# One state-space mixer: another order for the last subtractions, merged parameter loads, and three small moves

## The chip, the cores and the metric

The kernel runs on one core of a Trainium2 chip. The metric is the device time of one execution in microseconds (us), lower is better. The core has four engines that matter here: PE (TensorE, matrix products; its weight loads are listed apart as PEld), DVE (VectorE), ACT (ScalarE) and POOL (GpSimd). SP (SyncE), ACT and POOL also issue DMA transfers, which 16 DMA engines carry out. Each engine executes its own instructions in one fixed order; semaphores tie the engines together.

## The reference

One inference step of a small streaming encoder with two layers, width D = 1024, over 1024 prompt positions without history and 64 sample positions with a carried state. Each layer is a token mixer between RMS norms, then a gated feed-forward net with a causal depthwise convolution. Layer 0 mixes with sliding-window attention, layer 1 with a diagonal complex state-space model (S5), which is the part that the change touches:

```python
def s5_mixer(h, h0_re, h0_im, lam_re, lam_im, log_dt, b_re, b_im, c_re, c_im, d_skip, w_glu, b_glu):
    ...                       # u: h by 64 groups of 16 channels, state of 64 complex numbers a group
        xr = jnp.einsum('blgi,gpi->blgp', u_blk, bbr)      # and xi with bbi: inputs of the state
        ...                                                # the carried state enters at the first position
        _, _, sr, si = lax.associative_scan(_affine_combine, (ar, ai, xr, xi), axis=1)
        y = jnp.einsum('blgp,gip->blgi', sr, cr) - jnp.einsum('blgp,gip->blgi', si, ci)
    ...
    z = jax.nn.gelu(y + d_skip * h)
    ag = z @ w_glu + b_glu
    out = ag[..., :D_MODEL] * jax.nn.sigmoid(ag[..., D_MODEL:])
    return out, hr, hi
```

All of it is float32. The outputs are both activations, the attention cache rows, the final states and the last convolution rows.

## The kernel before, in words

The 1088 positions lie on the free axis, in three blocks of 384, 384 and 320 columns; the width is eight tiles of 128 partitions, kt = 0 to 7. A float32 product is made of three products of a high and a low part: high x low, high x high, low x high (`mm3`, lines 420 to 422; in the GLU line 1701). For a weight tile ACT copies the high part (line 406) and DVE subtracts it from the raw tile to get the low part (line 407); raw tiles have two buffers, and a new load (lines 383, 389) waits until both have read the old one. The order of every engine and of SP's queue is written out by hand in a table of numbers, `PINS`, and made binding by `pin`: an instruction that is not ready holds up all behind it on its engine.

**The mixer** (`ssm`) runs over 32 pairs of groups q, two to a batch except for the first two and the last two. The parameters of two pairs make one tile t of 16 (`pm`; `pm0` for t = 0 and 6), loaded by SP in `load`, one transfer of 522 KB for each pair. A batch does:

- PE, line 1506: the inputs of the state from U (the normed activations by groups, four tiles, scaled by DVE at line 1440) into `p1`;
- ACT, lines 1514 and 1518: a copy of sines `sc`, and the decays `rd` (mask times a number);
- DVE and POOL: `wk` is the state's work tile. DVE multiplies (1539, 1545), adds (1546), scans (1557), multiplies (1560, 1561); POOL zeroes the first column (1538) and copies the carried state `h0` in (1543) before line 1546;
- PE, lines 1569 and 1575: the direct part and the output of the states into `p3`;
- ACT, line 1583: `p3` into `ys`; after four pairs ACT's queue stores `ys` to memory (1589), SP loads it back transposed as `yf` (1595), ACT makes z by GELU (1609, 1612) and its high part `zh` (1620).

For the two batches of t = 0 (q = 0 and 1), line 1571 has PE do an idle product (`fill`, line 427) beside; it writes spare columns of a `p1` bank and nobody reads it.

**The end of the mixer.** The low parts `zl` of z (line 1636, function `lower`) are subtracted on DVE: 24 subtractions, eight tiles kt times three blocks. `lows` makes those of kt 0 to 5, after the low parts of two held weight tiles. `fo`, line 1649, sums the final state, and POOL stores it (1650).

**The GLU** (`tile_`) has eight output tiles m, for three blocks each; `pb` and `pa` are the PSUM sums of gate and value, from six buffers. For m = 0 the products come in four steps, each for all three blocks: high x high of kt 0 to 4; the products of kt 0 to 4 with a low part; kt 5 and 6; kt 7. Then the sigmoid on ACT (1716) and the product on DVE (1717) empty the two sums. Beside it POOL loads (1661), DVE adds and subtracts (1665 to 1668) and POOL stores (1669) sums of weights for the next net (`sj`), for which the small tiles of `t4` (five slots, shared by `ys`, `yf`, `z`, `sg` and `sj`) are used.

Of the kernel before, what the change touches and what calls it, by code (L numbers as in the profile page):

```python
# [203 lines left out]
class Core:  # L204
# [1237 lines left out]
    def ssm(self, after):  # L1442
# [4 lines left out]
        with tc.tile_pool(name="ss", bufs=1) as sp:  # L1447
# [47 lines left out]
            def batch(qs):  # L1495
# [91 lines left out]
                if qs[-1] % 4 == 3:  # L1587
# [33 lines left out]
                    if kt < 6:  # L1621
                        zs[kt] = z
                        return
# [266 lines left out]
```

## Time and profile before

| | |
|---|---|
| median of three runs | 2237.05 us (2235.64 to 2237.27) |
| profiled execution: its own time | 2237.79 us |
| its span | 2236.0 us |
| mean granted PE clock | 0.992 |
| instructions | 35979 |
| mixer, from the first line-1539 product to the last scan step | 1185.0 to 1268.2 us |
| GLU, from its first product | 1272.0 us on |

Rows of a timeline have the start in us from the span's start, the duration, engine, line, operation, the tile written and those read, the number of instructions in the row and, in brackets, how long the engine stood before it and what released it. A window row has busy time and number of instructions by engine, then the granted PE clock, the mean share of the 16 DMA engines that was busy (it can read over 1), and GB/s. Matmul ends are modelled, so their starts are more exact than their ends.

### The profile page before, as it was taken

What the parts mean: (1) busy time and instruction counts of PE and PEld (TensorE: products, weight loads), DVE (VectorE), ACT (ScalarE), POOL (GpSimd) and SP (SyncE); (2) the same over time, 40 slices, a digit from 0 to 9 for tenths busy, and PEclk for the clock granted to TensorE, in tenths of its full rate; (3) what the DMA queues carried; (4) which work ended last, traced back from release to release, by engine and by line L of the source; (5) the groups of instructions that cost most, each with busy time, mean ns of one, the idle gap of its engine ahead of it and who ended that gap; (6) DMA issues with size and microseconds to landing.
All of it is one profiled execution on the core that took longest, in us unless ns stands there. A gap on an engine that the chain in (4) does not pass through costs nothing.

```text
span 2236.0 us, 35979 instructions
## 1 busy us (share of the span) xinstructions
PE 2190.7 (98%) x13867; PEld 2116.8 (95%) x13867; DVE 1646.0 (74%) x2886; ACT 1046.0 (47%) x1865; POOL 423.1 (19%) x504
## 2 busy tenths in 40 slices
PE   9999999999999999999998899999999999999999
PEld 9987799999999999999986789999999999999998
DVE  8688648989878787767767765397977777677763
ACT  6256756422333332555543821263544445455543
POOL 4322005100122424001102244151021111110000
PEclk9999999999999999999999989999999999999999
DMA  5010015656255565887749878251378686578773
GB/s 208 26 30 21 20 62 177 234 202 211 91 152 173 194 206 173 287 272 232 248 172 354 255 271 301 103 180 63 113 260 277 225 293 229 197 271 307 224 252 101
DMA packets 208123, 428.47 MB, mean 192 GB/s; under 512 B 23312, under 2 KB 114224, under 8 KB 205008
## 3 DMA queue, kind: packets, MB, share of 16 engines
q1 hardware_dynamic: 175648, 326.56, 44.2%
q0 software_dynamic: 23984, 95.12, 12.0%
q10 hardware_dynamic: 8320, 4.49, 0.8%
q8 instruction: 109, 1.79, 0.3%
q14 instruction: 62, 0.51, 0.1%
HBM read 297.75 MB, written 128.37 MB: 191 GB/s over the span
## 4 chain that ended last, share of the span: by engine, by line
PE 73%; DMA 10%; DVE 9%; ACT 3%; issue 3%; POOL 1%; SPq 0%; ACTq 0%; DVEq 0%; POOLq 0%
PE mm L420 17%; PE mm L421 17%; PE mm L422 17%; PE pa L1701 4%; PE pb L1701 4%; DMA raw<-in_w_down 2%; PE po L1037 2%; DMA jw<-in_w_down 1%; PE tps L1030 1%; PE sps L1007 1%; PE p L1575 1%; DVE whl L407 1%; PE gq L420 1%; PE gq L422 1%; PE gq L421 1%
## 5 line engine op out<-in xcount | busy, mean ns | idle before, releaser
L420 PE MATMUL mm<-hl,whl 128*128 128x384 f32 (+1 forms) x1960 | 643.1, 329 | 3.1 <-DVE hl L504 2.0
L421 PE MATMUL mm<-hh,whl 128*128 128x384 f32 (+1 forms) x1960 | 643.1, 328 | 0.0
L422 PE MATMUL mm<-hh,whl 128*128 128x384 f32 (+1 forms) x1960 | 640.7, 328 | 0.4 <-DVE whl L407 0.4
L420 PEld LDWEIGHTS mm<-hl,whl 128*128 128x128 f32 x1960 | 368.5, 188 | 5.6 <-DVE hl L504 3.1
L422 PEld LDWEIGHTS mm<-hh,whl 128*128 128x128 f32 x1960 | 368.4, 188 | 0.9 <-DVE whl L407 0.7
L421 PEld LDWEIGHTS mm<-hh,whl 128*128 128x128 f32 x1960 | 368.7, 188 | 0.1
L407 DVE TENSOR_TENSOR whl<-raw,whl 128x1024 fp32r<-128x1024 f32 x201 | 250.6, 1249 | 138.8 <-ACT whl L406 138.5
L406 ACT ACTIVATE whl<-raw 128x1024 fp32r<-128x1024 f32 x201 | 212.0, 1058 | 282.7 <-PE mm L422 128.6
L420 PE MATMUL mm<-gt,whl 128*128 128x384 f32 (+1 forms) x968 | 317.1, 328 | 0.8 <-DVE y L843 0.5
L421 PE MATMUL mm<-gt,whl 128*128 128x384 f32 (+1 forms) x968 | 316.1, 327 | 0.0
L422 PE MATMUL mm<-gt,whl 128*128 128x384 f32 (+1 forms) x968 | 315.8, 327 | 0.0
L420 PEld LDWEIGHTS mm<-gt,whl 128*128 128x128 f32 x968 | 181.7, 188 | 1.5 <-DVE y L843 0.9
L421 PEld LDWEIGHTS mm<-gt,whl 128*128 128x128 f32 x968 | 181.7, 188 | 0.0
L422 PEld LDWEIGHTS mm<-gt,whl 128*128 128x128 f32 x968 | 181.6, 188 | 0.0
L373 DVE TENSOR_TENSOR whl<-raw,whl 128x1024 fp32r<-128x1024 f32 x84 | 96.5, 1154 | 75.2 <-ACT whl L372 74.8
L372 ACT ACTIVATE whl<-raw 128x1024 fp32r<-128x1024 f32 x84 | 82.7, 987 | 102.1 <-DMA raw<-sd 42.3
L648 ACT ACTIVATE t<-u,ppt 128x1090 f32<-128x1090 f32 x88 | 114.2, 1298 | 34.3 <-DVE u L747 23.5
L649 DVE SCALAR_TENSOR_TENSOR t<-u,ppt,t 128x1090 f32<-128x1090 f32 x88 | 125.9, 1431 | 5.3 <-ACT t L648 3.8
L650 DVE SCALAR_TENSOR_TENSOR t<-u,ppt,t 128x1090 f32<-128x1090 f32 x88 | 121.9, 1385 | 0.4
L640 DVE TENSOR_TENSOR u<-rb,mm 128x384 f32<-128x384 f32 (+1 forms) x164 | 80.6, 503 | 34.1 <-PE mm L422 29.3
L663 ACT ACTIVATE t<-t 128x1090 f32<-128x1090 f32 x44 | 49.1, 1116 | 119.1 <-DVE t L650 119.0
L793 DVE TENSOR_TENSOR gt<-gr,gt 128x768 fp32r<-128x768 f32 (+2 forms) x106 | 90.4, 880 | 10.9 <-ACT gt L792 10.2
(400 smaller groups left out, 4072.1 us busy)
## 6 DMA issues: line engine op xcount, KB each, us to landing
raw<-in_w_up SPq DMA_DIRECT2D x88, 512.0 KB, 4.4
raw<-in_w_down SPq DMA_DIRECT2D x74, 512.0 KB, 4.5
raw<-sd SPq DMA_DIRECT2D x40, 512.0 KB, 4.5
sj<-in_w_up POOLq DMA_DIRECT2D x68, 256.0 KB, 5.9
su<-sj POOLq DMA_DIRECT2D x34, 512.0 KB, 5.4
raw<-su SPq DMA_DIRECT2D x34, 512.0 KB, 4.7
pm<-prm SPq DMA_DIRECT2D x32, 522.0 KB, 8.4
gr<-td SPq DMA_DIRECT2D x40, 384.0 KB, 5.5
```

The lines of the kernel that those rows point to most:

```text
L372: nc.scalar.activation(w[:, 0], raw, AF.Copy)
L373: nc.vector.tensor_sub(w[:, 1], raw, w[:, 0].bitcast(F32))
L406: x = [nc.scalar.activation(w[:, 0], raw, AF.Copy)]
L407: low = lambda: nc.vector.tensor_sub(w[:, 1], raw, w[:, 0].bitcast(F32))
L420: nc.tensor.matmul(out, w[:, 0, sl], xl, start=start, stop=False, skip_group_check=more)
L421: nc.tensor.matmul(out, w[:, 0, sl], xh, start=False, stop=False, skip_group_check=more)
L422: self.last_mm = nc.tensor.matmul(out, w[:, 1, sl], xh, start=False, stop=stop, skip_group_check=more)
L648: nc.scalar.activation(t, u[:, 0:T + 2], AF.Identity, bias=cb(m), scale=cw(0, m))
L649: nc.vector.scalar_tensor_tensor(t, u[:, 1:T + 3], cw(1, m), t, op0=ALU.mult, op1=ALU.add)
L650: self.last_conv = nc.vector.scalar_tensor_tensor(t, u[:, 2:T + 4], cw(2, m), t, op0=ALU.mult, op1=ALU.add)
L793: nc.vector.tensor_sub(x[:, 1, u], raw, x[:, 0, u].bitcast(F32))
L1701: nc.tensor.matmul(ps[:, :n], w[:, e, k * P:(k + 1) * P], x[b][:, k], start=k == 0 and j == 0, stop=k == KD - 1 and j == 2)
```

## The change

Five edits, all in the mixer and its hand-written order.

1. The low parts of tile kt = 7 stood first among DVE's last subtractions; they stand last now, behind the 18 of kt 0 to 5, the sum `fo` and kt 6.
2. From t = 4 on, the parameters of two pairs come in one load of 1044 KB: 12 loads in place of 24.
3. The initial state h0 gets a tile of its own in a pool that is open from the kernel's start, instead of one in the mixer's pool.
4. On ACT the four decays of the first two batches' tiles stand behind the two small copies of lines 1421 and 1422.
5. The two idle products of line 427 are left out.

From line 1469 on the changed kernel's lines are one higher than before, from the middle of `batch` (1577) three lower, and from `lower` (1630) on one lower. The tables of numbers change in most of their rows, since fewer instructions are numbered, and are cut here.

```diff
@@ PINS @@
...
@@ load @@
-                for e in range(2):
-                    got[t] = nc.sync.dma_start(pm[:, e], self.prm[:, 2 * t + e])
+                k = 1 if t < 4 else 2
+                for e in range(0, 2, k):
+                    got[t] = nc.sync.dma_start(pm[:, e:e + k], self.prm[:, 2 * t + e:2 * t + e + k])
@@ ssm @@
-            h0 = sp.tile([P, NPR, 2], F32, name="h0")
+            h0 = self.small.tile([P, NPR, 2], F32, name="h0", bufs=1)
             nc.gpsimd.dma_start(h0, a["s_h0"])
@@ batch @@
-                    f = self.fill(p1s[-1][:, 0, 2 * NC_:], 1, 512 - 2 * NC_, x) if t == 0 else None
...
-                                if f is not None:
-                                    self.order(x, f)
-                                    f = None
...
                     if kt < 6:
                         zs[kt] = z
                         return
+                    yield
                     if kt < 7:
+                        lows()
+                    else:
                         yield
-                        lows()
                     for b in range(3):
                         x = lower(b, kt, z)
```

The rows of the following lists are instructions in the order of one engine: line, operation, tile written and tiles read with their buffer numbers, size, and the semaphores waited for. First DVE's order at the end of the mixer, before. `whl` is a weight tile of the GLU; `z_12521` is kt 7, `zs_11974`, `zs_12152` and `z_12378` hold kt 0 to 5 two by two, and `zl_12042`, `zl_12045`, `zl_12048` are blocks 0, 1 and 2:

```order
L407 TENSOR_TENSOR whl_12425<-raw_12423,whl_12425 128x1024 [waits DMAHW6_49]
L1636 TENSOR_TENSOR zl_12042<-z_12521,zh_12041 128x384 [waits Activation_49]
L1636 TENSOR_TENSOR zl_12045<-z_12521,zh_12044 128x384 [waits Activation_49]
L1636 TENSOR_TENSOR zl_12048<-z_12521,zh_12047 128x320 [waits Activation_49]
L1636 TENSOR_TENSOR zl_12042<-zs_11974,zh_12041 128x384 x2
L1636 TENSOR_TENSOR zl_12042<-zs_12152,zh_12041 128x384
L1636 TENSOR_TENSOR zl_12042<-z_12378,zh_12041 128x384 x2
```

The same place with the change, where kt 7 is `z_12507`, kt 6 `z_12501` and kt 4 and 5 are `z_12364`:

```order
L407 TENSOR_TENSOR whl_12411<-raw_12409,whl_12411 128x1024 [waits DMAHW2_49]
L1635 TENSOR_TENSOR zl_12031<-zs_11964,zh_12030 128x384 x2
L1635 TENSOR_TENSOR zl_12031<-zs_12139,zh_12030 128x384 x2
L1635 TENSOR_TENSOR zl_12031<-z_12364,zh_12030 128x384 [waits Activation_49]
L1635 TENSOR_TENSOR zl_12034<-zs_11964,zh_12033 128x384 x2
...
L1648 TENSOR_TENSOR fo_12539<-fin_11554 128x128 [waits Pool_49]
L1635 TENSOR_TENSOR zl_12031<-z_12501,zh_12030 128x384 [waits Activation_49]
...
L1635 TENSOR_TENSOR zl_12031<-z_12507,zh_12030 128x384 [waits Activation_49]
```

The wait for the last tile moved from the head of the 24 to its end. Next POOL's order at the mixer's start, before and then with the change (`h0` carried state, `mask` the tile that the decays are made from, `wk` the first batches' work tiles):

```order
L1487 DMA h0_11554<-in_s_h0 128x64 [waits DMAHW0_49,DVE_49,DMAHW5_49,PE_49,DMAHW7_49,Activation_49,Pool_49]
L1491 MEMSET mask_11557 128x138
L1538 MEMSET wk_11571 128x2
...
L1492 MEMSET mask_11557 128x1 [waits Pool_49]
L1493 MEMSET mask_11557 128x1
L1543 COPY wk_11571<-h0_11554 128x2 [waits DMASW6_49,DVE_49]
```

```order
L1488 DMA h0_11552<-in_s_h0 128x64
L1492 MEMSET mask_11555 128x138 [waits DMAHW0_49,DVE_49,DMAHW5_49,PE_49,DMAHW7_49,Activation_49,Pool_49]
L1539 MEMSET wk_11569 128x2
...
L1493 MEMSET mask_11555 128x1 [waits Pool_49]
L1494 MEMSET mask_11555 128x1
L1544 COPY wk_11569<-h0_11552 128x2 [waits DMASW6_49,DVE_49]
```

The wait for the end of the layer boundary moved from the load to the memset behind it. Last, ACT's order around the second store of `ys`, before and then with the change; the numbers at the semaphores DMAHW are those that SP's and ACT's transfers count up in turn:

```order
L1583 ACTIVATE ys_11784<-p3_11820 128x2x137 [waits PE_49]
L1589 DMA yd_11520<-ys_11784 128x8x137 [waits DMAHW2_49,Activation_49]
L1514 ACTIVATE sc_11863<-pm0_11590 128x2x138 [waits DMAHW7_49,DMAHW6_49,DVE_49]
L1514 ACTIVATE sc_11863<-pm0_11590 128x2x138
L1518 ACTIVATE rd_11864<-mask_11557,rho_296 128x276 x2
```

```order
L1580 ACTIVATE ys_11777<-p3_11812 128x2x137 [waits PE_49]
L1586 DMA yd_11520<-ys_11777 128x8x137 [waits DMAHW3_49,Activation_49]
L1515 ACTIVATE sc_11854<-pm0_11588 128x2x138 [waits DVE_49]
L1515 ACTIVATE sc_11854<-pm0_11588 128x2x138
L1519 ACTIVATE rd_11855<-mask_11555,rho_296 128x276 x2
```

The store waited for semaphore 2, which counts a load of t = 8; it waits for semaphore 3 now, which counts the load of `pm0` for t = 6, the tile that the next instruction reads.

118 rows, old and new, of the table PINS are left out of this document.

## The prediction

> **What bounds the kernel now.** I read the page first, then the PE's waits in the two halves of layer 1, then the timelines of the places where the change lies.
>
> ```profile
> span 2236.0 us, 35979 instructions
> ...
> PE 2190.7 (98%) x13867; PEld 2116.8 (95%) x13867; DVE 1646.0 (74%) x2886; ACT 1046.0 (47%) x1865; POOL 423.1 (19%) x504
> ```
>
> PE is busy 98% of the span, so an edit pays only where PE stands or runs slowly. The PE's waits from 1180 to 1296 us (mixer and start of the GLU), in us, times and longest, and then from 1296 us to the end:
>
> ```profile
> PE pb L1701 <- DVE zl L1636: 13.8, 2, 10.0
> ...
> PE mm L420 <- DVE u L746: 3.8, 4, 1.5
> ```
>
> The largest wait of the second half is 3.8 us in 940: it is bound by PE's own products, so what PE gains before it should arrive at the end in full. The largest of the first half, 13.8 us, lies in the GLU's first output tile (m = 0). Its place in the timelines (start us, duration, count at the end, in brackets the idle time before it), PE's rows first, then DVE's:
>
> ```profile
> 1277.02 0.34 PE L1701 MATMUL pb<-zh,whl 128*128 128x384 f32 x1
> 1287.32 0.69 PE L1701 MATMUL pb<-zl,whl 128*128 128x384 f32 x1 [9.96 <-DVE zl L1636]
> ...
> 1292.81 0.69 PE L1701 MATMUL pb<-zl,whl 128*128 128x384 f32 x1 [3.85 <-DVE zl L1636]
> ...
> 1312.81 0.51 PE L1701 MATMUL pb<-zh,whl 128*128 128x384 f32 x2
> ...
> 1270.09 2.36 DVE L407 TENSOR_TENSOR whl<-raw,whl 128x1024 fp32r<-128x1024 f32 x2 [1.94 <-ACT whl L406]
> 1285.37 1.43 DVE L1636 TENSOR_TENSOR zl<-z,zh 128x384 fp32r<-128x384 f32 x3 [12.92 <-ACT zh L1620]
> 1286.71 1.49 DVE L1636 TENSOR_TENSOR zl<-zs,zh 128x384 fp32r<-128x384 f32 x3
> ...
> 1291.40 2.23 DVE L1636 TENSOR_TENSOR zl<-zs,zh 128x320 fp32r<-128x320 f32 x5
> ```
>
> PE has done the 30 high-by-high products and needs the first low part at 1277.2. DVE is free from 1272.45, yet stands 12.92 us before the three lows of tile 7, whose high parts ACT makes last (rows below). The 18 lows that PE wants, and whose inputs are there, are queued behind them. PE then starts m = 1 at 1312.81.
>
> **The change part by part. The reordered tail.** The same 24 subtractions stay; only their order changes. From 1285.37 to 1286.71 DVE takes three of them, two of 384 columns and one of 320: 1.34 / 3 = 0.45 us each. From 1272.45 on, five apiece, block 0's are ready at 1274.7, block 1's at 1277.0, block 2's at 1279.2, tile 5's three at 1280.6, the sum of the final state and tile 6's at about 1282.2. ACT's rows say when the highs exist:
>
> ```profile
> 1278.37 1.28 ACT L1620 ACTIVATE zh<-z 128x384 fp32r<-128x384 f32 x3
> ...
> 1284.83 1.28 ACT L1620 ACTIVATE zh<-z 128x384 fp32r<-128x384 f32 x3
> 1286.01 1.99 ACT L406 ACTIVATE whl<-raw 128x1024 fp32r<-128x1024 f32 x2
> 1307.11 2.16 ACT L406 ACTIVATE whl<-raw 128x1024 fp32r<-128x1024 f32 x2 [19.11 <-DMA raw<-in_w_glu]
> 1309.28 1.28 ACT L1716 ACT_TABLE_LOAD   x1
> 1310.58 0.58 ACT L1716 ACTIVATE sg<-pb,ppt 128x384 f32<-128x384 f32 x1
> ```
>
> Tile 6's highs are ready at 1279.65 and the earlier tiles' before that, tile 7's at 1286.1; so DVE waits for tile 7 alone and ends it at about 1286.6. PE does not stop at 1277.2. What it has left of m = 0 takes, from the chain of waits (start, duration, count):
>
> ```profile
> 1297.65 1.74 PE pb L1701 x10
> ...
> 1301.15 1.46 PE pb L1701 x10
> ...
> 1280.00:1284.00 4.00, 0.00 (x0) 0.00 (x0) 0.00 (x0) 1.30 (x1) 0.00 (x0) 0.51 0.98 347
> ```
>
> 40 products of 0.174 and 20 of 0.146 are 9.9 us, to 1287.1; the 36 of tiles 5 and 6 are 24 x 0.174 + 12 x 0.146 = 5.9, to 1293.0; the 18 of tile 7 are 3.0, to 1296.0. Each block's lows are there before PE comes to it, tile 7's 6 us before. The window (its last three columns are granted clock, DMA share, GB/s) shows that PE's stop also halves its clock; 13 products after the stop run at 0.32 us instead of 0.17. That goes with it. Against 1312.81 the tail could give 16.8 us.
>
> But something is late next: m = 1 takes over the PSUM that m = 0's sigmoid empties, and the sigmoid stands on ACT behind the high copies of m = 2's two weight tiles. Their loads and what runs beside them (SP and POOL timelines, then the time to landing of those two loads, and the page's row of the same size of load):
>
> ```profile
> 1297.54 1.54 SPq L389 DMA_DIRECT2D raw<-in_w_glu  x2
> ...
> 1295.01 4.27 POOL L1661 DMA_DIRECT2D sj<-in_w_up  x6 [0.18 <-issue]
> ...
> DMA to landing us min/median/max: 9.4/9.5/9.5
> ...
> raw<-sd SPq DMA_DIRECT2D x40, 512.0 KB, 4.5
> ```
>
> They can go when DVE has taken m = 1's lows: right behind tile 7, with ACT's copies of 1286.01, so about 1288.3 instead of 1297.5. They take 9.5 us beside six loads of 256 KB on POOL, 4.5 us in the other row. POOL's loads follow the store of the final state, which now comes before tiles 6 and 7; part of them will be over, so I take 5.5, nearer to the lower: landing 1293.8. ACT's copies 2.2, table load 1.3 and sigmoid 0.6 bring 1297.9, and m = 1 starts near 1298: 15 us gained. With 9.5 us it starts at 1302 (-11), with a landing that hides wholly at 1296 (-16.8). **A = -15, bounds -11 to -16.8.**
>
> **The mixer's head and loads.** Four edits, one place:
>
> ```profile
> 1187.03 0.44 DVE L1546 TENSOR_TENSOR wk<-wk 128x274 f32<-128x274 f32 x1 [1.20 <-POOL wk L1543]
> ...
> 1195.53 0.72 DVE L1539 TENSOR_TENSOR wk<-pm,p 128x548 f32<-128x548 f32 x1 [1.60 <-issue]
> ...
> 1190.96 0.85 PE L427 MATMUL p<-ppt,ident 128*128 128x238 f32 x2 [1.84 <-DVE wk L1539]
> ...
> 1181.83 1.77 ACT L1518 ACTIVATE rd<-mask,rho 128x276 f32<-128x276 f32 x4 [1.40 <-POOL mask L1493]
> ...
> 1217.99 0.76 ACT L1514 ACTIVATE sc<-pm 128x276 f32<-128x276 f32 x2 [4.86 <-DMA pm<-prm]
> ...
> 1218.78 0.72 DVE L1545 TENSOR_TENSOR wk<-sc,p 128x548 f32<-128x548 f32 x1 [2.90 <-ACT sc L1514]
> 1219.42 0.49 DVE L1440 TENSOR_TENSOR U<-U,sel 128x328 f32<-128x328 f32 x1
> ```
>
> The initial state's load no longer waits for the layer boundary, so the 1.20 us go. Putting the small copies before the four decays lets U be scaled earlier: the decays hold ACT for 1.77 us from 1181.83, and I count half, 0.9, since the copies must also wait for PE's sums. The decays are needed only at the first scan, past 1187. The two idle products are short, but the p1 bank they write makes them wait 1.84 us for DVE and DVE later stand 1.60: with both gone DVE is 1.20 + 0.9 + 1.7 = 3.8 us ahead at the third batch.
>
> Before 1218 ACT stands 4.86 us at its store of ys, and DVE 2.90 behind it. The store shares a DMA semaphore with a parameter load that is due later; with 12 loads fewer the numbers shift and the store shares one with the pair that ACT's next instruction wants anyway. That wait goes too. What is late next is the third U tile and then the later parameters, whose issue and landing are:
>
> ```profile
> L1432 SPq DMA_DIRECT2D U<-hd x1: 371/371/371, 1203.8 to 1203.8; - x1
> ...
> DMA to landing us min/median/max: 10.3/10.3/10.3
> ...
> L1470 SPq DMA_DIRECT2D pm<-prm x2: 320/663/1006, 1240.2 to 1240.6; - x2
> ...
> DMA to landing us min/median/max: 8.1/8.8/9.5
> ...
> 1192.00:1196.00 4.00, 3.42 (x32) 2.91 (x32) 2.40 (x5) 1.93 (x6) 0.10 (x1) 0.66 1.09 388
> ...
> 1232.00:1236.00 4.00, 4.00 (x52) 3.47 (x53) 4.00 (x7) 3.97 (x5) 1.50 (x4) 1.00 0.61 213
> 1236.00:1240.00 4.00, 4.00 (x50) 3.29 (x44) 3.91 (x6) 3.48 (x11) 1.40 (x3) 1.00 0.88 284
> ...
> 1249.47 0.62 PE p L1506 x8
> ```
>
> U lands at 1214.1, where DVE scales it at 1219.42 now: at most 5.3 us ahead. After that the 16 DMA engines decide. They are full (share over 1.0) at nearly all times from 1180 on (the window of 1192 is one), and idle only 0.39 x 4 + 0.12 x 4 = 2.0 us between 1232 and 1240. The two loads of 1240 land by 1250.1, and PE takes the first half at 1249.47: it is at their heels. An earlier mixer can pull these loads forward by that idle time and by little more, so I carry 2.4 us of the 5.3, nearer to the idle time than to U. The merged load moves the same bytes, but its first half now counts as landed with the second: PE would wait from 1249.47 to 1250.1, +0.6, and that is the other end if nothing is pulled forward. **B = -2.4, bounds +0.6 to -5.3.**
>
> The Trainium skill, "DMA: Bandwidth & Descriptors", section "Anatomy of one DMA — SWDGE (gpsimd) path", puts about 2.0 us of fixed time on each DMA, and its section "Bandwidth" asks for 1 MiB or more in each. By it 12 loads fewer would free some 24 us of queue time, by an estimate from that page, and B would go to -5.3, the rival of the whole head below. The full share in the rows above speaks against it: the fixed parts overlap already.
>
> **The sum.** -15.0 - 2.4 = -17.4 on the profiled execution's 2237.79 us is 2220.4. That execution lies 0.74 above the median of 2237.05; against the median it is 2219.6, say **2219.5 us**.
>
> **Rivals.**
>
> *The mixer gives nothing.* If the loads after 1240 are bound by the DMA engines from the start, the head's gain is given back at the thirteenth load: B about 0, A as it stands, 2222. For it: the full share; against it: the 2 us of idle engines.
>
> *The sigmoid is the new wall.* The m = 2 loads still take 9.5 us because POOL's six loads move earlier as much as they do: A = -11, with B 2223.6. For it: ACT's 19.11 us before those copies. Against it: POOL's loads are released by a store that now lies before six lows.
>
> *The whole head is carried.* The loads are issued by slots that come free earlier, and U decides: B = -5.3, at A = -15 to -16.8 that is 2215 to 2217. For it: SP issues each load when a slot is free; against it: the share.
>
> *The other side: each merged pair stalls.* Every one of the 12 batches whose parameters came in the second half of a split now waits for 522 KB more; at the 284 GB/s of the window above that is 1.84 us each, 22 us in all, and 17.4 are won: 2242. It decides if PE reaches each pair as it lands, from 1.5 us a pair up. Against it: PE is busy 4.00 of 4 us in both windows from 1232 to 1240, with loads under way.
>
> *The change does nothing:* the lows keep waiting, if ACT's highs or slots of the shared small pool hold the 18 back: 2237. Only the later tiles' highs are late, so I hold it for very unlikely.
>
> **How the numbers follow.** Forecast 0.61, no gain in the mixer 0.13, sigmoid wall 0.12, whole head 0.09, stalling pairs 0.03, nothing 0.02. The least gain of the first four is 11 - 0.6 = 10.4 (2226.7), the largest 16.8 + 5.3 = 22.1 (2215); if U does not hold the head back, its gains are 3.8 + 2.9 = 6.7 instead of 5.3 (2213.5). The range is 2213 to 2227. What can be told from no change is about 0.2%, 4.5 us; the first four cases, 0.95, lie beyond it: faster 0.95, same 0.02, slower 0.03.
>
> **What would show it.** Right: the PE's wait for the lows near 1277 falls from 13.8 us to under 1, DVE's wait of 12.92 shrinks to some 3 and stands before tile 7, the window at 1280 to 1292 shows clock 1.00, and m = 1 starts 15 us earlier after the end of m = 0 less about 2 us of wait for the sigmoid. The 4.86 us of ACT before 1218 and the 1.20 of DVE are gone. Wrong: a wait of PE for sg above 4 us, waits for pm at most batches, or a second half that takes longer than its 940 us now.

## The result, and the profile after

The changed kernel takes 2224.60 us (median of four runs, 2221.95 to 2229.22) against 2237.16 (2235.64 to 2238.74): 0.9946 of the kernel before, 95% interval 0.9928 to 0.9964. That is 12.6 us less, where 17.4 was forecast (2219.5 us). The time lies in the stated range; the likeliest case was too good by 5 us. The profiled execution took 2225.26 us.

The page of the changed kernel, and PE's waits from 1170 to 1320 us (us in total, times, longest):

```profile
span 2223.5 us, 35945 instructions
...
PE 2187.6 (98%) x13863; PEld 2116.2 (95%) x13863; DVE 1648.5 (74%) x2886; ACT 1046.7 (47%) x1865; POOL 425.3 (19%) x504
```

```profile
PE pb L1700 <- ACT sg L1715: 5.8, 1, 5.8
PE p L1507 <- DMA pm<-prm: 2.7, 2, 1.5
...
PE pr L464 <- DVE sqa L458: 1.6, 1, 1.6
```

The 13.8 us of waiting for the lows are gone. A wait of 5.8 us for the sigmoid stands in their place. The PE timeline shows where (start, duration, in brackets the idle time before; the first row is the GLU's first product, the last but one the first of m = 1, the last the first of m = 2):

```profile
1267.02 1.15 PE L1700 MATMUL pb<-zh,whl 128*128 128x384 f32 x5 [0.81 <-ACT ys L1580]
...
1272.09 0.33 PE L1700 MATMUL pb<-zh,whl 128*128 128x384 f32 x1
1272.26 0.33 PE L1700 MATMUL pb<-zl,whl 128*128 128x384 f32 x1
...
1290.75 0.31 PE L1700 MATMUL pa<-zl,whl 128*128 128x320 f32 x1
1296.83 1.01 PE L1700 MATMUL pb<-zh,whl 128*128 128x384 f32 x2 [5.77 <-ACT sg L1715]
...
1322.63 0.51 PE L1700 MATMUL pb<-zh,whl 128*128 128x384 f32 x2
```

PE runs from the high-by-high products into the low ones without a stop and ends m = 0 at 1291.06, 24.0 us after the GLU's first product; in the kernel before that took 41. DVE, ACT, then the loads of POOL and of SP (timelines), and last the time to landing of the two of line 389:

```profile
1278.37 1.43 DVE L1635 TENSOR_TENSOR zl<-z,zh 128x384 fp32r<-128x384 f32 x3 [1.29 <-ACT zh L1617]
1280.10 2.36 DVE L407 TENSOR_TENSOR whl<-raw,whl 128x1024 fp32r<-128x1024 f32 x2 [0.29 <-ACT whl L406]
```

```profile
1279.02 1.99 ACT L406 ACTIVATE whl<-raw 128x1024 fp32r<-128x1024 f32 x2
1291.72 1.06 ACT L406 ACTIVATE whl<-raw 128x1024 fp32r<-128x1024 f32 x1 [10.71 <-DMA raw<-in_w_glu]
1293.82 1.06 ACT L406 ACTIVATE whl<-raw 128x1024 fp32r<-128x1024 f32 x1 [1.05 <-DMA raw<-in_w_glu]
1294.90 1.28 ACT L1715 ACT_TABLE_LOAD   x1
1296.19 1.06 ACT L1715 ACTIVATE sg<-pb,ppt 128x384 f32<-128x384 f32 x2
```

```profile
1276.86 4.26 POOL L1660 DMA_DIRECT2D sj<-in_w_up  x6
```

```profile
1278.33 0.89 SPq L515 DMA_DIRECT2D xl<-x  x2
1281.35 1.48 SPq L389 DMA_DIRECT2D raw<-in_w_glu  x2
```

```profile
DMA to landing us min/median/max: 10.3/10.8/11.3
```

DVE waits 1.29 us for tile 7 instead of 12.92. Block 0 of m = 0 could have its sigmoid from about 1288.6 on, when the last of its products into pb ends; ACT stands 10.71 us before m = 2's weights instead, which were asked for at 1281.35 and 1282.5 and land at 1291.7 and 1293.8. The stop costs a second time through PE's clock (windows of 2 us; the last three columns are granted clock, DMA share, GB/s):

```profile
1294.00:1296.00 2.00, 0.00 (x0) 0.00 (x0) 1.45 (x3) 1.98 (x2) 0.00 (x0) 0.54 0.53 133
1296.00:1298.00 2.00, 1.17 (x4) 1.17 (x5) 1.93 (x6) 1.24 (x3) 0.31 (x1) 0.50 0.75 254
1298.00:1300.00 2.00, 2.00 (x8) 2.00 (x7) 1.48 (x3) 1.47 (x2) 2.00 (x4) 0.50 0.91 340
1300.00:1302.00 2.00, 2.00 (x11) 2.00 (x10) 0.94 (x2) 1.06 (x1) 2.00 (x4) 0.76 0.87 234
```

In the mixer the 4.86 us of ACT at the store are gone, and another wait has come later:

```profile
1213.96 0.76 ACT L1515 ACTIVATE sc<-pm 128x276 f32<-128x276 f32 x2 [0.78 <-DVE wk L1562]
...
1225.41 0.69 ACT L1580 ACTIVATE ys<-p 128x274 f32<-128x274 f32 x2 [5.50 <-DMA yd<-ys]
...
1233.53 1.16 PE L1507 MATMUL p<-U,pm 128*64 128x137 f32 x16 [1.51 <-DMA pm<-prm]
```

**Where the time went.** Four places are marked in both traces: DVE's first `sel` of line 1418 (the mixer's start, before any edit acts), the GLU's first product, the first product of m = 2, and the end of the span. Before they stand at 1181.34, 1271.97, 1336.59 and 2236.0; after at 1179.26, 1267.02, 1322.63 and 2223.5.

| stretch | before | after | difference |
|---|---|---|---|
| to the mixer's start (no edit here) | 1181.3 | 1179.3 | -2.1 |
| mixer, to the GLU's first product | 90.6 | 87.8 | -2.9 |
| GLU, to m = 2's first product | 64.6 | 55.6 | -9.0 |
| rest (no edit here) | 899.4 | 900.9 | +1.5 |

So the two stretches of the change give 11.9 us in this execution. The other two are what one execution differs from another. The mixer term was forecast at -2.4, the GLU term at -15.0, with bounds of -11 and -16.8: the gap is in the second, and its -9.0 lies outside these bounds.

### The profile page after: what moved, and what is told of

Its sections match the earlier page's. It is cut to its first block, busy times and chain, and to the rows that moved or that the text cites. A ratio compares the mean times of both kernels' runs of the same rounds, so it can differ in the third digit from the quotient of the medians.

```text
span 2223.5 us, 35945 instructions
## 1 busy us (share of the span) xinstructions
PE 2187.6 (98%) x13863; PEld 2116.2 (95%) x13863; DVE 1648.5 (74%) x2886; ACT 1046.7 (47%) x1865; POOL 425.3 (19%) x504
## 3 DMA queue, kind: packets, MB, share of 16 engines
q0 software_dynamic: 23984, 95.12, 11.9%
## 4 chain that ended last, share of the span: by engine, by line
PE 82%; DVE 6%; DMA 6%; issue 2%; ACT 2%; POOL 0%; SPq 0%; ACTq 0%; DVEq 0%; POOLq 0%
PE mm L420 21%; PE mm L422 21%; PE mm L421 21%; PE pb L1700 4%; PE pa L1700 4%; PE po L1037 2%; PE tps L1030 1%; PE sps L1007 1%; PE gq L420 1%; PE gq L422 1%; PE gq L421 1%; DMA raw<-in_w_down 1%; DVE whl L407 1%; DMA yd<-ys 1%; PE go L420 1%
## 5 line engine op out<-in xcount | busy, mean ns | idle before, releaser
L1700 PE MATMUL pb<-zh,whl 128*128 128x384 f32 (+1 forms) x384 | 96.1, 332 | 6.6 <-ACT sg L1715 5.8
## 6 DMA issues: line engine op xcount, KB each, us to landing
pm<-prm SPq DMA_DIRECT2D x12, 1044.0 KB, 11.4
```

Of the source, the lines that this page charges most:

```text
L1700: nc.tensor.matmul(ps[:, :n], w[:, e, k * P:(k + 1) * P], x[b][:, k], start=k == 0 and j == 0, stop=k == KD - 1 and j == 2)
```

## Experiments

In the table at the end of this section the mixer and the GLU stretch are measured between the same marks for all of them, one profiled execution each, and the issue of m = 2's first weight load is counted from the GLU's first product; the ratios are of the times.

**The tail alone, and all but the tail.** `tail_alone` is the kernel before with the new order of the lows; `tail_undone` the changed kernel with the old order.

```diff
 # tail_undone; tail_alone is the kernel before with the reverse
-                    yield
                     if kt < 7:
-                        lows()
-                    else:
                         yield
+                        lows()
```

> The kernel before with the reordered last subtractions alone; loads, initial state, decays and idle products as before. Theory (the reorder's gain is cut by a new wait for the sigmoid): PE's 13.8 us wait for the lows is gone, a wait for sg of 5 to 6 us stands before m = 1, and the kernel takes about 9 us less than before, 2228. Rival (the reorder gives its full 15 us and the mixer's edits cost 3): about 2222.

> The changed kernel with the old order of the last subtractions. Theory: the mixer's four edits together give about 2.9 us, 2234, and the 13.8 us wait for the lows is back. Rival (the mixer's edits cost time): 2237 or more.

Times: 0.9933 (0.9909 to 0.9958), 2223.61 us, and 0.9978 (0.9967 to 0.9989), 2232.63 us, both against 2236.38. PE's waits, of `tail_alone` and then of `tail_undone`:

```profile
PE pb L1703 <- ACT sg L1718: 2.6, 1, 2.6
...
PE p L427 <- DVE wk L1539: 0.9, 1, 0.9
```

```profile
PE pb L1698 <- DVE zl L1633: 12.1, 2, 8.3
PE p L1507 <- issue: 2.2, 1, 2.2
```

The mixer's edits without the tail's are worth 3.75 us by the medians, 4.9 by the ratio (mixer stretch 88.1 against 90.6): the rival by which they cost time falls. The reorder by itself gives as much as the whole change, 12.8 us by the medians and 15.0 by the ratio, and not the 9 that were expected, so the number of the rival was nearer, though not its reason. Its GLU stretch is 50.6, with a wait of 2.6 us for the sigmoid and no loss of clock, where the changed kernel had 5.8 us and half clock. The wait itself is there, but its length is not the 5.8 us of one profile.

**The sigmoid first.** If the sigmoid of block 0 need not stand behind m = 2's weights, the wait must go. Two moves in the order tables:

```diff
 # ACT
+L1715 sg(m=0, block 0)
 L406 whl(m=2) x2
-L1715 sg(m=0, block 0)
 # DVE
+L1716 y(m=0, block 0)
 L407 whl(m=2) ...
-L1716 y(m=0, block 0)
```

> The changed kernel; on ACT the sigmoid of block 0 of m = 0 stands ahead of the two weight copies of m = 2, and on DVE its product ahead of their low parts. Theory: the 5.8 us wait for sg falls under 1.5 us, PE keeps its clock, and the kernel takes 6 to 8 us less than the changed one, 2217 to 2219. Rival (m = 1 waits for something else as long, its weights or DVE): 2223 or more.

> The kernel with the sigmoid of block 0 ahead once more, with more rounds, to tell it from the changed kernel: 6 to 8 us less than the changed one, that is 0.990 to 0.992 of the kernel before. If the first look was luck of transfers that landed early, 0.994 to 0.995.

Times: 0.9914 (0.9893 to 0.9934), 2218.29 against 2236.38, and again 0.9934 (0.9916 to 0.9951), 2221.81 against 2236.45. By these ratios it lies 3 to 10 us below the changed kernel (0.9946 and 0.9957), which was measured in other series; the expected 6 to 8 us are within that, and the second series fell short of its 0.992. The interval of that series overlaps those of the changed kernel, and its value is that of `tail_alone`, so the times alone do not show the gain. In the trace it is plain. ACT and then PE of `sigmoid_first`:

```profile
1281.18 1.28 ACT L1715 ACT_TABLE_LOAD   x1
1288.26 0.58 ACT L1715 ACTIVATE sg<-pb,ppt 128x384 f32<-128x384 f32 x1 [5.79 <-PE pb L1700]
1288.74 1.05 ACT L406 ACTIVATE whl<-raw 128x1024 fp32r<-128x1024 f32 x1
```

```profile
1290.36 0.31 PE L1700 MATMUL pa<-zl,whl 128*128 128x320 f32 x1
1290.51 0.51 PE L1700 MATMUL pb<-zh,whl 128*128 128x384 f32 x2
```

The table load falls into idle time, the sigmoid waits for PE and no longer the reverse, and m = 1 follows m = 0 without a gap. The GLU stretch is 47.6 us in both profiles of it, 17.0 below the kernel before: the 16.8 that the prediction had as the reorder's full worth, if nothing new is waited for.

**What makes m = 2's weights late.** Four runs: the changed kernel once more, and three that move what stands ahead of the two loads.

> The changed kernel once more, unaltered. It shows how far the wait for sg and the landing of m = 2's two weight loads (5.8 us; 10.4 and 11.3 us) differ between executions. Theory (the landing sets the wait, and it varies with what else the DMA engines carry): wait and landing differ from before and move together. Rival (the 5.8 us are fixed by instruction order): the wait is 5.8 us again within 0.5.

It took 0.9957 (0.9942 to 0.9973), 2231.10 us on a chip on which the kernel before had 2239.66. The time to landing of m = 2's two loads in it:

```profile
DMA to landing us min/median/max: 7.0/7.4/7.8
```

The same kernel has a wait of 5.8 us with a landing of 10.3 and 11.3, and one of 4.2 with 7.0 and 7.8: the order of instructions doesn't fix it, and the rival falls. The two loads were issued at another time, too: 14.3 us after the GLU's first product there and 16.2 here.

```diff
 # sums_late: DVE
-L1648 fo
 L1635 zl (kt 6, kt 7)
 L407 whl(m=1) x2
+L1648 fo
 # residual_behind: SP
+L389 raw<-in_w_glu (m=2) x2
 L515 xl<-x x2
-L389 raw<-in_w_glu (m=2) x2
 # weights_ahead: both
```

> The changed kernel; on DVE the sum of the final state stands behind the low parts of m = 1's weights, so that POOL's store of it and the six loads of weight sums behind it start after the two weight loads of m = 2. Theory (those six loads made the two late): their time to landing falls from 10.4 and 11.3 us to 5 to 7, the wait for sg from 5.8 to under 2, 2217 to 2220. Rival (the two loads are slow by themselves): landing stays at 9 us or more and the wait at 4 or more, 2223 to 2225.

> The changed kernel; SP issues the two weight loads of m = 2 ahead of the two residual loads xl, which wait for the store of the final state. Theory (bytes ahead in the DMA queues make the weight loads late): 0.79 MB fewer ahead, landing 2 us earlier, 8 to 9 us, wait for sg 3 to 4 us, 2220 to 2222. Rival (the order does not matter, landing is 10 us anyway): 2224.

> The changed kernel with both: the two weight loads of m = 2 ahead of the residual loads on SP, and the sum of the final state behind the low parts of m = 1's weights on DVE, so that POOL's six loads of weight sums come after the weight loads. Theory (what stands ahead in the DMA queues makes them late): landing 4.5 to 6 us, wait for sg under 1 us, 2216 to 2219. Rival (they are slow by themselves): landing 9 us or more, wait 4 us or more, 2223 or more.

Times: `sums_late` 0.9957 (0.9937 to 0.9977), `residual_behind` 0.9934 (0.9912 to 0.9956), `weights_ahead` 0.9950 (0.9932 to 0.9967). First `sums_late`, whose landing (9.6 and 10.5 us) did not fall. SP's timeline shows why:

```profile
1280.96 0.89 SPq L515 DMA_DIRECT2D xl<-x  x2
1281.94 1.15 SPq L389 DMA_DIRECT2D raw<-in_w_glu  x2
```

The experiment missed its aim. The raw buffers were free at 1278.4, but the two residual loads `xl` stand ahead on SP, and they go only when the store of the final state has landed (issued at 1279.06, 1.8 us). Holding the sum back held SP's queue back too, and the six loads of POOL were again ahead. The other two, `residual_behind` and then `weights_ahead`, by the time to landing:

```profile
DMA to landing us min/median/max: 4.6/5.4/6.2
```

```profile
DMA to landing us min/median/max: 3.4/3.8/4.2
```

With the residual loads behind, the two weight loads land in 4.6 and 6.2 us, with POOL's loads behind as well in 3.4 and 4.2. The landing also depends on how long after POOL's six the two are issued, and that differs between executions: they wait for the low parts of tile 7, which DVE starts 11.4 us after the GLU's first product in the changed kernel and 14.5 in `residual_behind`. Runs with like times of issue can be compared by the table below: 3.4 and 4.2 stand against 7.0 and 7.2 in `tail_alone` (issued at 15.4 and 15.2 us), and 4.6 and 6.2 against 7.1 and 7.2 in `more_bytes` (17.4 and 17.0). So what stands ahead in the DMA queues makes them late: six loads of 256 KB and two of 384, 2.3 MB. That part of the theory is shown, by one profile for each order.

The wait follows less well: it is 3.8 us in both. In all nine profiles in which PE waits for sg before m = 1, PE starts 3.0 us after ACT begins to copy the second of the two tiles, so issue and landing together set the wait. In `residual_behind` the landing is 5 us shorter than in the changed kernel, but the issue is 3.1 us later. In `weights_ahead` PE starts m = 1 without a stop and then waits for pa. What releases it is the sigmoid of block 1, before which ACT stands for 7.12 us, and not DVE's products of m = 0, which start only when PE runs again. The rows there of DVE, ACT, PE and again DVE:

```profile
1299.31 0.42 DVE L1664 TENSOR_TENSOR sj<-sj 128x256 f32<-128x256 f32 x1 [8.14 <-DMA sj<-in_w_up]
...
1305.32 0.58 ACT L1715 ACTIVATE sg<-pb,ppt 128x384 f32<-128x384 f32 x1 [7.12 <-DVE whl L407]
1305.95 1.01 PE L1700 MATMUL pa<-zh,whl 128*128 128x384 f32 x2 [3.75 <-ACT sg L1715]
1306.49 1.82 DVE L1716 SCALAR_TENSOR_TENSOR y<-pa,ppt,sg 128x384 f32<-128x384 f32 x3
```

The low part of a weight tile that the profile names as ACT's releaser stands on DVE behind the sums of the loads that were just made late. The store of the first of these sums lands at nearly the same time (issued at 1301.76, 3.4 us), so which of the two held the sigmoid stays open. Either way the wait comes from the loads that were put behind, and the time that was expected did not come.

**The mixer's four edits.** `loads_split` gives every pair its own load again, `head_undone` undoes the other three, and `more_bytes` adds three copies from memory to memory that nothing reads.

```diff
 # loads_split
-                for e in range(0, 2, k):
-                    got[t] = nc.sync.dma_start(pm[:, e:e + k], self.prm[:, 2 * t + e:2 * t + e + k])
+                for e in range(2):
+                    got[t] = nc.sync.dma_start(pm[:, e], self.prm[:, 2 * t + e])
 # more_bytes, in batch
+                if qs[0] in (8, 12, 16):
+                    more = self.dram.tile([P, 2, PRM], F32, name=f"more{qs[0]}")
+                    nc.gpsimd.dma_start(more, self.prm[:, qs[0]:qs[0] + 2])
```

> The changed kernel with the parameters of t = 4 on again in one load for each pair of groups. Theory: the store of ys shares its semaphore with a later load again, ACT stands 3 to 5 us at it and DVE 2 to 3 us behind; yet by the first product of the GLU at most 1 us is lost, since the later waits for parameters take it in: 2224 to 2226. Rival (the merged load is itself what gains, by fixed costs saved): the GLU begins 2 to 3 us later, 2227 or more; or (the halves arriving earlier help) it begins earlier, 2222 or less.

> The changed kernel with split loads once more. In the two profiles with split loads and the new order of the tail, the m = 2 weight loads landed 23.4 and 23.5 us after the GLU's first product and m = 2 began at 50.6 and 51.9; in four profiles with merged loads it was 25.1 to 26.7 and 54.4 to 55.6. If the merging causes this: 23 to 24 and 50 to 52 again, and a time of 0.994 or less of the kernel before. If it is the spread of the landing between executions: anything from 23 to 27, and 0.994 to 0.997.

> The changed kernel with the three small moves at the mixer's start undone (initial state in the mixer's pool, the decays ahead of the small copies, the two idle products); merged loads and the tail's order stay. Theory (from the middle of the mixer on its transfers decide, so an earlier head is worth little at its end): counted from the mixer's first sums, the third U slice but one (the fifth of eleven) is scaled 3 us later, as before the change, and the GLU's first product comes at most 1.5 us later than in the changed kernel, the time within 1.5 us of it. Rival (the head is carried to the end): the GLU begins 3 us later, and the kernel takes 3 us more.

> The changed kernel; POOL issues three more copies from memory to memory, of 1.07 MB each, in the batches of pairs 8, 12 and 16, which nothing reads. Theory (the mixer's second half is bound by its transfers): parameters come later, PE's waits for them grow from 2.7 us to over 6, and the time from the mixer's start to the GLU's first product grows by 5 to 15 us from 88. Rival (bound by DVE, transfers hidden): under 1.5 us more.

Times: `loads_split` 0.9940 (0.9919 to 0.9961) and again 0.9938 (0.9919 to 0.9957), `head_undone` 0.9952 (0.9937 to 0.9968), and `more_bytes` 2237.75 us in its single run. ACT and DVE of `loads_split` around the store of ys:

```profile
1216.07 0.37 ACTq L1585 DMA_DIRECT2D yd<-ys  x1
1216.56 0.76 ACT L1514 ACTIVATE sc<-pm 128x276 f32<-128x276 f32 x2 [6.40 <-DMA U<-hd]
```

```profile
1217.35 0.72 DVE L1545 TENSOR_TENSOR wk<-sc,p 128x548 f32<-128x548 f32 x1 [3.21 <-ACT sc L1514]
```

The wait at the store is back, 6.40 us with 3.21 behind it, as expected (the profile names a load of U as what ended it, where before it named one of pm). In the middle of the mixer it costs: the fifth of the eight U rows in DVE's timeline comes 35.3 us after the mixer's start, against 32.3 in the changed kernel. Yet the mixer stretch is 87.4 and 88.1 us, no longer than with merged loads: by its end the merge gives nothing that its missing store wait would promise. For `head_undone` the expectation counts eleven slices of U, and the trace has nine, in eight rows. The third row comes 14.9 us after the mixer's start, against 13.8 in the changed kernel and 16.7 before, the fifth 33.3 against 32.3 and 38.1: 1.1 us later in both, where 3 were expected. Even that is not clear of the spread, since `tail_undone`, with the same head as the changed kernel, has its third row at 12.3. The stretch is 88.7, 0.9 longer, less than the spread between executions. PE's waits of `more_bytes`, where 3.2 MB more go through the mixer:

```profile
PE p L1507 <- issue: 5.6, 1, 5.6
PE p L1507 <- DMA pm<-prm: 3.8, 2, 3.0
```

Of the expected 6 us of waiting for pm 3.8 go by that name; the 5.6 beside them the profile does not assign, and `sigmoid_again`, without these copies, has a wait of 4.6 us of the same kind. The stretch grows by 9.4 us to 97.2, which is 3.2 MB at 340 GB/s, close to the 364 GB/s that they move on average from 1180 to 1240 us of the changed kernel. So the DMA engines have no room for these bytes, and the mixer is bound by transfers from there on; the rival by which DVE bounds it falls. It adds load and doesn't take any away, so how long the mixer would be with early parameters was not tried.

| kernel | mixer | issue of m = 2's weights | their landing | wait for sg | GLU to m = 2 |
|---|---|---|---|---|---|
| before | 90.6 | 25.6 | 9.4, 9.5 | - | 64.6 |
| tail_alone | 90.3 | 15.2 | 7.0, 7.2 | 2.6 | 50.6 |
| tail_undone | 88.1 | 23.9 | 8.8, 8.9 | - | 63.3 |
| changed | 87.8 | 14.3 | 10.3, 11.3 | 5.8 | 55.6 |
| changed_again | 91.7 | 16.2 | 7.0, 7.8 | 4.2 | 54.4 |
| head_undone | 88.7 | 14.8 | 9.4, 9.7 | 4.6 | 55.1 |
| loads_split, split_again | 87.4, 88.1 | 15.0; 14.9 | 7.2; 7.7, 8.1 | 2.4; 3.2 | 51.9, 53.7 |
| sums_late | 86.1 | 18.8 | 9.6, 10.5 | 8.9 | 59.1 |
| residual_behind | 88.4 | 17.4 | 4.6, 6.2 | 3.8 | 53.2 |
| weights_ahead | 89.3 | 15.4 | 3.4, 4.2 | 3.8 (pa) | 54.4 |
| sigmoid_first, sigmoid_again | 87.8, 89.8 | 14.9; 15.9 | 7.2, 7.3; 6.9, 7.8 | 0 | 47.6, 47.6 |
| more_bytes | 97.2 | 17.0 | 7.1, 7.2 | 4.4 | 55.1 |

## Why the prediction was right or wrong

**The lows' order: right to a tenth.** The prediction had DVE wait for tile 7 alone and PE end m = 0 24.0 us after the GLU's first product. Both came so, and where the sigmoid was put first the stretch fell by 17.0 against 16.8.

**The loads of m = 2: the step that failed.** The prediction took 5.5 us to landing, out of 4.5 and 9.5, on the ground that part of POOL's loads would be over, and a stall of 2 us. Measured are 7 to 11 us and 2.4 to 5.8; a wait for sg above 4 us was the prediction's own sign of being wrong. The reorder frees the store of the final state and with it POOL's six loads and SP's two residual loads, which the prediction did not count at all; all eight are issued just ahead of the weights, and `weights_ahead` shows 3.4 and 4.2 us without them. They stood just ahead in the kernel before, too, and the 9.5 us that the prediction read there were the price with them. The rival that the prediction named "the sigmoid is the new wall", 2223.6 us, is what happened, and it had 0.12. Its reason was right too: counted from the GLU's first product, POOL's loads begin 13.2 us earlier and the weights' 11.2. That its time is within 1 us of the measured one is in part luck, since it holds no loss of clock.

**The clock: left out.** The prediction saw that PE's stop halves its clock in the kernel before and booked the gain, but did not ask the same of the new stop. In the changed kernel m = 1 takes 25.8 us from its first product to that of m = 2, in `sigmoid_first`, without a stop, 23.8. These 2.0 us and the 4.0 by which m = 1 starts later than forecast (29.8 us after the GLU's first product instead of 25.8) are the whole gap of 15.0 - 9.0 = 6.0.

**The mixer: right in size, as far as the spread lets it be seen, and for its reason.** -2.4 forecast, -2.9 in the first profile; over the eight profiles with all four edits the stretch is 86.1 to 91.7, mean 88.6, against 90.6 and 90.3 without: -1.9. A single profile, with a spread of 5.6 us, would not show it. In the batch for which the prediction had DVE 3.8 us ahead it is 2.8 ahead. The U slice of the fifth row is scaled 32.3 us after the mixer's start instead of 38.1; the prediction's bound from U's landing, 1214.1 less 1181.3, was 32.8. From there transfers decide, as `more_bytes` shows. The wait at the store did go, and ACT met 5.50 us more at the next buffer of ys, whose store took 17.1 us to land.

**The merged loads.** With split loads the mixer is not longer (87.4 and 88.1 us against 87.8). The Trainium skill, "DMA: Bandwidth & Descriptors", section "Anatomy of one DMA — SWDGE (gpsimd) path", would by its 2 us for each load, which it fits to loads issued by POOL and not by SP as here, have given it more; the trace decides against that sum here. With a new order of the tail, the three profiles with split loads have GLU stretches of 50.6 to 53.7, the four with merged loads and nothing else moved in the GLU 54.4 to 55.6. From the mixer's start to m = 2 that makes 139.3 to 141.8 us with split loads and 143.4 to 146.1 with merged ones (`more_bytes` left aside), and the ratios, 0.9933 to 0.9940 against 0.9946 to 0.9957, point the same way with intervals that overlap. But with the sigmoid first, ACT begins to copy m = 2's second tile 23.4 and 24.8 us after the GLU's first product though the loads are merged; with split loads that is 23.5 to 24.2, in the other four 25.2 to 26.8. So nothing shows that merging gains, and whether it costs the GLU 2 us stays open.

**The sum.** In time the mixer's edits can be told only while the old tail stands (0.9978). With the new tail, 0.9933 without them and 0.9946 and 0.9957 with them are one value. In the traces the gain of the mixer is lost in the GLU stretch (87.8 and 55.6 us against 90.3 and 50.6 in `tail_alone`). Why is argued only: an earlier mixer ends at the same wait for loads.

## What to carry to other kernels

When a wait is taken out, list what its end used to release, on every queue, and what is then issued together: here it was one sum, which freed a store; six loads stood behind the store and two waited for it, and all eight went ahead of the two that the next step needed. An activation that frees PSUM belongs ahead of copies that wait for a transfer; here that order shortened the GLU stretch more than any shortening of the transfer (47.6 us against 53.2 and 54.4). Price a new stop of PE with the clock it loses.

## What the runs showed of the hardware

What a stop costs PE in clock does not follow from its length alone. In all fourteen traces the recorded changes of the granted clock lie on a grid of 3.41 us: every stretch at 0.50 lasts one or more whole steps, but for the last of a trace. In `loads_split` a stop of 2.42 us leaves PE busy for 1.36 us of one step, and the clock falls to 0.50 at the end of that step, 1.36 us after PE had started again at full pace. In `tail_alone` a stop of 2.58 us is divided between two steps, with 1.91 and 2.34 us busy, and the clock stays at 1.00. In the changed kernel, with a stop of 5.77 us, it is at 0.50 for two steps, of which some 4 us lie behind the restart. So it matters where on the grid a stop falls. The busy share at which the clock falls can't be read from these traces: from full clock, steps with shares up to 0.77 were followed by half clock and steps with shares down to 0.49 were not (matmul ends are modelled). First `loads_split`, then `tail_alone`, in windows cut along the grid:

```profile
1294.50:1297.91 3.41, 1.36 (x8) 1.36 (x9) 3.34 (x8) 2.44 (x4) 0.30 (x1) 1.00 0.88 247
1297.91:1301.33 3.42, 3.42 (x12) 3.42 (x11) 1.00 (x2) 0.83 (x2) 3.42 (x6) 0.50 0.99 387
```

```profile
1293.59:1297.00 3.41, 1.91 (x12) 1.64 (x11) 2.18 (x3) 2.97 (x3) 0.86 (x2) 1.00 1.05 375
1297.00:1300.42 3.42, 2.34 (x13) 2.35 (x14) 3.22 (x7) 2.01 (x4) 1.35 (x3) 1.00 0.82 276
1300.42:1303.83 3.41, 3.41 (x22) 3.41 (x21) 1.31 (x2) 2.03 (x2) 3.41 (x5) 1.00 0.94 351
```

The Trainium skill, "TensorE: Matmul & The Clock Gate", section "Why this matters for your kernels", warns of gaps over about 3 us; the 2.42 us here were enough once and the 2.58 were not.

And the same two loads of one program, with the same ones ahead, landed after 10.3 and 11.3 us in one execution and 7.0 and 7.8 in another. Part of that is the count's start: in the second they were issued 1.9 us later after the GLU's first product, and ACT began to copy the second tile 25.2 us after it instead of 26.8.
